# An encoder trunk on one core: the queue that stores kept differences, where down's first inputs are split, and three more seven-product pairs

## The chip, the cores and the metric

The kernel runs on one core of a Trainium2 chip. The metric is the device time of one execution in microseconds (us), less is better. The kernel before takes 2078.95 us, the median of three executions that took 2076.1, 2078.95 and 2083.54 us.

## What is computed

Two encoder layers over 256 tokens of width 2048, with an MLP of width 8192. Both layers have an attention sub-layer (differential attention in the first, windowed grouped attention in the second, each with four heads into a memory of 256 tokens) and a squared-ReLU MLP:

```python
for i in range(2):
    h = rms_norm(x, norm_attn[i])
    ...                                  # projections, attention, memory attention
    x = x + heads @ w_out[i]             # 2048 x 2048
    h = rms_norm(x, norm_mlp[i])
    x = x + jnp.square(jax.nn.relu(h @ w_up[i])) @ w_down[i]     # 2048 x 8192, 8192 x 2048
```

The change touches the MLP alone, which the kernel runs as a stage "up" (`h @ w_up`) and a stage "down".

## The kernel before, in words

**Products.** The matmuls take operands of a reduced type (`F32R`), so each float32 operand is split into a high part (a cast on ScalarE, ACT in the profile, line 442) and a low part (a subtraction on VectorE, DVE, line 443). One product is then three matmuls on TensorE (PE), high by high, high by low and low by high, each 128x128 by 128x512 (`three`, lines 534 to 536). Weights arrive in pieces of 128x1024. Two pieces make a pair, and a pair of plain form is eight products, so 24 matmuls.

**Seven-product pairs.** Some pairs are computed with seven products (`seven`, 21 matmuls) in the manner of Strassen. Such a pair, called fast here, needs sums of weights, which `sum_pair` makes on VectorE (lines 356 and 357, and `first_sum`, line 283) and splits into four parts `ah, al, bh, bl`; and differences of the inputs, which `differences` makes on VectorE (lines 545 to 548) and splits as well. `FAST` and `LATE` list which of the 32 pairs of each half of down are fast: `LATE` holds for the second half of the first layer's down, `FAST` for the three others. `LATE_BLK` lists those of `LATE` whose sums lie in the buffers `blk` and not in `x2`. The first sum of a fast pair in down is made ahead in DRAM by `make_sums`, with a copy (line 291) and an accumulating transfer (line 295) that GpSimd (POOL) issues while earlier stages run.

**Kept differences.** The input differences of a fast pair serve both halves of down. They are made once, while up makes the hidden values: `keep` takes a buffer `h2`, makes the differences, and stores them to DRAM in a transfer that GpSimd issues (line 1013). Down loads them again for each half (`load_kept`, line 1122, GpSimd). Hidden chunks 6 to 14 are also moved to DRAM by GpSimd (line 1037) and loaded by SyncE (SP).

**Order.** The program's text is not the order of the engines alone. Tasks such as `keep` are queued with a wait counted in ticks; the loop over pairs gives two ticks with each pair, at which due tasks are emitted (`Light(f, gap)` runs `f`, and the next step of the task follows `gap` ticks later). Buffers come from pools: `x2` has 8, `h2` 6, `blk` 10. A buffer is handed out again in turn, so an instruction that writes to a handed-out buffer waits until the last reader of it is done, a storing DMA among these. Each engine executes its instructions strictly in its own order, so whatever stands behind a waiting one waits too.

**Start of down.** Up ends with its last pair, the side sums `u`, and `to_hidden`, which transposes them on PE (line 1031) and applies relu and square on ScalarE (lines 1033, 1034). Down then splits its first input in `h2_of(0)` and starts.

Of the kernel before, what the change touches and what calls it, by code (L numbers as in the profile page):

```python
# [15 lines left out]
F32R = mybir.dt.float32r  # L16
# [6 lines left out]
P = 128  # L23
# [24 lines left out]
AHEAD = 2  # L48
WARM = 10
FAST = (2, 4, 6, 7, 9, 11, 12, 14, 16, 17, 19, 21, 22, 24, 26, 27, 29)  # L50
LATE = (2, 4, 6, 9, 11, 12, 14, 16, 19, 21, 24, 26, 29)
AWAY = range(6, 15)
LATE_BLK = (9, 12, 16, 21, 26)
LOOK = 3
KEEP_AFTER = (2, 6, 10, 14)
KEEP_LAST = (10, 18, 26, 34)
SUM_AT = {0: 44, 1: 2}
SUM_GAP = ({"in": 4, "mem": 4, "out": 4, "up": 11}, {"in": 4, "mem": 12, "out": 12, "up": 7})
LAM_INIT = 0.8 - 0.6 * math.exp(-0.3 * 0)
# [11 lines left out]
def trunk(ctx: ExitStack, tc: tile.TileContext, xin, xtok, memin, memtok, posrel, gcol, rows,  # L71
# [12 lines left out]
    def nm(s):  # L84
        uid[0] += 1
        return f"{s}{uid[0]}"
# [4 lines left out]
    def quad(tag, shape=(P, 2, 2, 256), dt=F32R):  # L91
        return xp.tile(list(shape), dt, tag=tag, name=nm(tag), bufs={"x2": 8, "h2": 6, "blk": 10}[tag])
# [904 lines left out]
    def mlp(layer, X2, last):  # L997
# [7 lines left out]
        def hidden(j):  # L1005
            return hT[j // 2].rearrange("p k s -> p (k s)")[:, (j % 2) * 512:(j % 2) * 512 + 512]

        def keep(j):

            t2 = quad("h2", (P, 2, 512))  # L1010
            differences(t2, hidden(j))
            kept[j] = dp.tile([P, 2, 512], F32R, name=nm("kept"))
            nc.gpsimd.dma_start(kept[j], t2)

        name = f"up{layer}"
        diffs = {}
# [6 lines left out]
        def to_hidden(q, n, u, i, tag):  # L1023
            c = 2 * q + n
            if i == 0:
                hT.append(wide[:, 5] if c == 15 else blk([P, 4, S], F32))
            pt = bank(tag)
            for oo in range(2):
                for t in range(2):
                    o = 2 * i + oo  # L1030
                    nc.tensor.transpose(out=pt[:, oo * S + t * P:oo * S + (t + 1) * P], in_=u[n][t][:, o * P:(o + 1) * P], identity=ident)  # L1031
            j = 2 * c + i
            nc.scalar.activation(hidden(j), pt, AF.Relu)
            nc.scalar.activation(hidden(j), hidden(j), AF.Square)
            if c in AWAY:
                hidden_in[j] = dp.tile([P, 512], F32, name=nm("hid"))
                nc.gpsimd.dma_start(hidden_in[j], hidden(j))
            if any(j in fast_pairs(f"down{layer}", h) for h in range(2)):
                Task([Light(lambda: keep(j), 0)], wait=KEEP_AFTER[2 * n + i] if q < 7 else KEEP_LAST[2 * n + i])

        for q in range(8):
            tag, other = ("mm", "aux") if q % 2 == 0 else ("aux", "mm")
            own = [[bank(tag) for _ in range(2)] for _ in range(2)]
            fast = UP_FAST[q]
            for j in range(8):
                if j == fast[0]:
                    side = [bank(other) for _ in range(4)]
                if q == 0 and j in DIFF_UP:
                    i = DIFF_UP[j]
                    diffs[i] = quad("h2" if i == 2 else "blk", (P, 2, 512))  # L1050
                    pair_differences(X2.pairs[i], diffs[i])
                two = [piece(name, q, 2 * j + i) for i in range(2)]
                pair = X2.pairs[j]

                def at(kk, t, part):
                    return pair[:, kk, part, t * P:(t + 1) * P]

                if j in fast:
                    seven(own, side, j == fast[0], j == fast[-1], two, sums.pop((name, q, j)), at, diffs[j])
                elif j < 7:  # L1060
                    for kk in range(2):
                        for t in range(2):
                            for n in range(2):
                                one_of_eight(own, n, t, 2 * j + kk, KT - 1, two, at)
                else:
                    for n in range(2):
                        for t in range(2):
                            for kk in range(2):
                                one_of_eight(own, n, t, 2 * j + kk, KT - 1, two, at)
                if j == fast[-1]:  # L1070
                    u = side_sums(side)
                for _ in range(2):
                    tick(2)
            own_add(own, u)
            if q == 0:
                mlp_stats()
            Task([lambda q=q, u=u, n=n, i=i, tag=tag: to_hidden(q, n, u, i, tag) for n in range(2) for i in range(2)], wait=1, gap=0)
        slots.append(blk([P, 4, S], F32))
        N2 = Halves()
        while making:  # L1080
            making.popleft()[1]()

        def h2_of(j):
            t2 = quad("h2", (P, 2, 512))
            split(t2[:, 0, :], t2[:, 1, :], hids.pop(j) if j in hidden_in else hidden(j))
            return lambda kk, t, part: t2[:, part, kk * S + t * P:kk * S + (t + 1) * P]

        for half_ in range(2):
            tag = "mm" if half_ == 0 else "aux"
# [32 lines left out]
                    nc.gpsimd.dma_start(diff_in[j], kept[j])  # L1122

            load_kept(1)
            ats = deque([h2_of(0)])
            for j in range(32):
                if j == fast[0]:
                    side = [bank("aux" if half_ == 0 else "mm") for _ in range(4)]
                two = [piece(f"down{layer}", half_, 2 * j)]
                if j < 31:  # L1130
                    ats.append(h2_of(j + 1))
                load_kept(j + 2)
                two.append(piece(f"down{layer}", half_, 2 * j + 1))
                at = ats.popleft()
# [184 lines left out]
```

## Time and profile before

| what | value |
|---|---|
| median of three executions | 2078.95 us |
| the profiled execution | 2079.43 us |
| its span in the profile | 2077.6 us, so 1.83 us lie outside it |
| TensorE busy, and its mean granted clock | 2068.8 us, 1.0 |
| VectorE, ScalarE, GpSimd busy | 1790.4, 1280.2, 193.2 us |
| DMA | 572.28 MB, mean 275 GB/s |
| up of the first layer, and of the second | about 404 to 764 us, 1402 to 1748 us |
| down of the first layer, first and second half | about 764 to 938 us, 938 to 1100 us |
| down of the second layer | about 1748 to 2077 us |

A row of a timeline gives the start in us, the duration, the engine, the line, the operation, and output<-inputs by the program's names, with partitions by elements. In brackets stands the engine's idle time just ahead of the row and what released it. A matmul is listed with 0.39 us, but matmuls overlap, so the distance between starts is what each costs. A row of the table by stretch holds the busy time of each engine in that stretch with the count of instructions, then the granted clock, the DMA share and GB/s. Rows of DMA issues give the count, the size and the median us from issue to landing.

### The profile page before, as it was taken

To read this page: it belongs to the slowest core of one execution; us is meant where nothing else is said; L and a number is where in the kernel's file an instruction comes from. 1 tells how busy PE (TensorE), PEld (TensorE's weight loads), DVE (VectorE), ACT (ScalarE), POOL (GpSimd) and SP (SyncE) were. 2 spreads that over 40 slices of the span, in tenths; PEclk is the share of its full clock that TensorE was granted. 3 is DMA by queue.
4 is the path that set the end of the run, shared out by engine and by line. 5 is a ranking of instruction groups with operands and counts; after the bars stand their busy time and mean duration, and the time that the engine had idled before them with its cause. 6 is when DMAs were issued, how large, how long until landed. Compare 5 with 4: busy or idle time off the path is not lost.

```text
span 2077.6 us, 28751 instructions
## 1 busy us (share of the span) xinstructions
PE 2068.8 (100%) x9996; PEld 1718.0 (83%) x9996; DVE 1790.4 (86%) x2583; ACT 1280.2 (62%) x1906; POOL 193.2 (9%) x301
## 2 busy tenths in 40 slices
PE   9999999999999999999999999999999999999999
PEld 7888888888888888888888888888888888888887
DVE  7677778898999999998886678889999889999998
ACT  7466665556655676666655556566556567766764
POOL 1201111100010010000001110000101111000000
PEclk9999999999999999999999999999999999999999
DMA  9678988877887789988978987568889998998994
GB/s 312 244 241 276 272 291 232 269 232 218 272 291 259 237 293 329 357 289 282 326 265 273 267 252 228 187 223 244 262 273 293 303 286 309 328 363 309 306 356 168
DMA packets 170641, 572.28 MB, mean 275 GB/s; under 512 B 19744, under 2 KB 20768, under 8 KB 169248
## 3 DMA queue, kind: packets, MB, share of 16 engines
q1 hardware_dynamic: 132976, 440.41, 59.8%
q0 software_dynamic: 37376, 130.04, 23.4%
q8 instruction: 78, 1.28, 0.2%
q14 instruction: 67, 0.55, 0.1%
q10 hardware_dynamic: 144, 0.01, 0.0%
HBM read 537.74 MB, written 97.65 MB: 306 GB/s over the span
## 4 chain that ended last, share of the span: by engine, by line
PE 92%; DMA 2%; DVE 2%; issue 2%; ACT 1%; SPq 0%; POOL 0%; ACTq 0%; DVEq 0%; POOLq 0%
PE mm L535 11%; PE mm L534 11%; PE mm L536 11%; PE aux L535 11%; PE aux L536 11%; PE aux L534 11%; PE mm L495 7%; PE mm L496 7%; PE mm L497 7%; DMA kept<-h 1%; DVE lo L443 1%; PE aux L638 1%; PE mm L1031 1%; PE aux L615 1%; PE aux L657 1%
## 5 line engine op out<-in xcount | busy, mean ns | idle before, releaser
L443 DVE TENSOR_TENSOR lo<-raw,hi 128x1024 fp32r<-128x1024 f32 (+1 forms) x512 | 607.6, 1207 | 168.3 <-ACT hi L442 166.7
L442 ACT CAST hi<-raw 128x1024 fp32r<-128x1024 f32 (+1 forms) x512 | 515.3, 1036 | 377.7 <-PE mm L497 113.9
L495 PE MATMUL mm<-hi,x 128*128 128x512 f32 x640 | 256.7, 403 | 0.7 <-ACT hi L442 0.7
L496 PE MATMUL mm<-lo,x 128*128 128x512 f32 x640 | 250.8, 392 | 0.0
L497 PE MATMUL mm<-hi,x 128*128 128x512 f32 x640 | 250.3, 391 | 0.0
L442 ACT CAST h<-big 128x1024 fp32r<-128x1024 f32 (+1 forms) x100 | 101.1, 1020 | 145.0 <-DVE big L283 90.2
L535 PE MATMUL aux<-lo,h 128*128 128x512 f32 x440 | 171.5, 390 | 0.2 <-DVE lo L443 0.2
L534 PE MATMUL aux<-hi,h 128*128 128x512 f32 x440 | 171.6, 390 | 0.0
L536 PE MATMUL aux<-hi,h 128*128 128x512 f32 x440 | 171.4, 389 | 0.0
L534 PE MATMUL mm<-hi,h 128*128 128x512 f32 (+1 forms) x438 | 170.1, 389 | 0.9 <-ACT h L442 0.9
L535 PE MATMUL mm<-lo,h 128*128 128x512 f32 (+1 forms) x438 | 169.8, 388 | 0.0
L536 PE MATMUL mm<-hi,h 128*128 128x512 f32 (+1 forms) x438 | 169.5, 388 | 0.0
L534 PE MATMUL mm<-hi,x 128*128 128x512 f32 x414 | 161.9, 391 | 0.0
L535 PE MATMUL mm<-lo,x 128*128 128x512 f32 x414 | 161.5, 390 | 0.2 <-DVE lo L443 0.2
L536 PE MATMUL mm<-hi,x 128*128 128x512 f32 x414 | 161.3, 390 | 0.0
L442 ACT CAST hi<-big 128x1024 fp32r<-128x1024 f32 (+1 forms) x146 | 128.9, 911 | 47.8 <-issue 24.5
L535 PE MATMUL aux<-lo,x 128*128 128x512 f32 x398 | 155.3, 390 | 0.5 <-DVE lo L443 0.5
L534 PE MATMUL aux<-hi,x 128*128 128x512 f32 x398 | 155.7, 391 | 0.0
L536 PE MATMUL aux<-hi,x 128*128 128x512 f32 x398 | 155.1, 390 | 0.0
L443 DVE TENSOR_TENSOR lo<-big,hi 128x1024 fp32r<-128x1024 f32 (+1 forms) x146 | 149.1, 1044 | 4.3 <-ACT hi L442 4.3
L497 PEld LDWEIGHTS mm<-hi,x 128*128 128x128 f32 x640 | 120.2, 188 | 26.0
L495 PEld LDWEIGHTS mm<-hi,x 128*128 128x128 f32 x640 | 120.5, 189 | 24.6 <-ACT hi L442 1.1
(310 smaller groups left out, 4268.6 us busy)
## 6 DMA issues: line engine op xcount, KB each, us to landing
raw<-in_w_up SPq DMA_DIRECT2D x164, 512.0 KB, 5.8
raw<-in_w_down SPq DMA_DIRECT2D x128, 512.0 KB, 5.6
madesum<-in_w_down POOLq DMA_DIRECT2D x124, 512.0 KB, 6.5
big<-in_w_up SPq DMA_DIRECT2D x92, 512.0 KB, 4.6
raw<-in_w_a SPq DMA_DIRECT2D x72, 512.0 KB, 4.7
h<-kept POOLq DMA_DIRECT2D x64, 512.0 KB, 5.9
big<-in_w_down SPq DMA_DIRECT2D x54, 512.0 KB, 5.2
big<-madesum SPq DMA_DIRECT2D x53, 512.0 KB, 5.3
```

The lines of the kernel that those rows point to most:

```text
L442: nc.scalar.copy(hi, src)
L443: return nc.vector.tensor_tensor(lo, src, as32(hi), op=ALU.subtract)
L495: nc.tensor.matmul(ps[t], lhsT=xh, rhs=hi[:, ws], start=(k == 0), stop=False)
L496: nc.tensor.matmul(ps[t], lhsT=xh, rhs=lo[:, ws], start=False, stop=False)
L497: nc.tensor.matmul(ps[t], lhsT=xl, rhs=hi[:, ws], start=False, stop=(k == KT - 1))
L534: nc.tensor.matmul(acc_, lhsT=x(0), rhs=w2[0][:, ws], start=first_, stop=False)
L535: nc.tensor.matmul(acc_, lhsT=x(0), rhs=w2[1][:, ws], start=False, stop=False)
L536: nc.tensor.matmul(acc_, lhsT=x(1), rhs=w2[0][:, ws], start=False, stop=last_)
L615: nc.tensor.transpose(out=pt[:, h * P:(h + 1) * P], in_=qn[t][:, h * P:(h + 1) * P], identity=ident)
L638: nc.tensor.transpose(out=pt[:, kt * S + qt * P:kt * S + (qt + 1) * P], in_=p_of(qt)[:, kt * P:(kt + 1) * P], identity=ident)
L657: nc.tensor.matmul(ps[c][:, qt * S:(qt + 1) * S], lhsT=qT[a][r, hl, qs], rhs=kT[b][r, hl, :], start=(a + b == 0), stop=(a == 1))
L1031: nc.tensor.transpose(out=pt[:, oo * S + t * P:oo * S + (t + 1) * P], in_=u[n][t][:, o * P:(o + 1) * P], identity=ident)
```

## The change

Three edits, all in the MLP.

First, `LATE` goes from 13 to 16 pairs: 17, 22 and 27 are added, so that the second half of the first layer's down has fast pairs next to each other at 16 and 17, 21 and 22, 26 and 27, as the other halves have. All halves together go from 64 to 67 fast pairs. `LATE_BLK` is chosen anew. The built program has 9 matmuls fewer, 6 casts more on ScalarE and 12 operations more on VectorE; six more transfers make the three sums in DRAM, three more load them and three more load kept differences.

Second, `keep` makes the differences as before, but the store is a step of its own, two ticks (one pair) later, and ScalarE issues it (`nc.scalar.dma_start`, line 1017 of the changed kernel) instead of GpSimd. There are 34 such stores.

Third, the first input of each half of down is split sooner. That of the first half, `h2_of(0)`, is emitted at the last pair of up (q = 7, j = 7), before its pieces; that of the second half at the last pair of the first half.

```diff
-LATE = (2, 4, 6, 9, 11, 12, 14, 16, 19, 21, 24, 26, 29)
+LATE = (2, 4, 6, 9, 11, 12, 14, 16, 17, 19, 21, 22, 24, 26, 27, 29)
-LATE_BLK = (9, 12, 16, 21, 26)
+LATE_BLK = (9, 12, 16, 19, 22, 26, 29)
+KEEP_GAP = 2
...
-        def keep(j):
-
-            t2 = quad("h2", (P, 2, 512))
-            differences(t2, hidden(j))
-            kept[j] = dp.tile([P, 2, 512], F32R, name=nm("kept"))
-            nc.gpsimd.dma_start(kept[j], t2)
+        def keep(j, wait):
+
+            def make():
+                box.append(quad("h2", (P, 2, 512)))
+                differences(box[0], hidden(j))
+
+            def store():
+                kept[j] = dp.tile([P, 2, 512], F32R, name=nm("kept"))
+                nc.scalar.dma_start(as32(kept[j]), as32(box.pop()))
+
+            box = []
+            Task([Light(make, KEEP_GAP), Light(store, 0)], wait=wait)
...
-                Task([Light(lambda: keep(j), 0)], wait=KEEP_AFTER[2 * n + i] if q < 7 else KEEP_LAST[2 * n + i])
+                keep(j, KEEP_AFTER[2 * n + i] if q < 7 else KEEP_LAST[2 * n + i])
...
+                if q == j == 7:
+                    ats = deque([h2_of(0)])
                 two = [piece(name, q, 2 * j + i) for i in range(2)]
...
-            ats = deque([h2_of(0)])
             for j in range(32):
...
-                if j < 31:
-                    ats.append(h2_of(j + 1))
+                if j < 31 or half_ == 0:
+                    ats.append(h2_of((j + 1) % 32))
```

What moves on the engines is seen at three places. In the names, `hi` and `lo` are the parts of a weight piece, `h2` and `x2` the buffers of those pools, `mm` and `aux` the accumulators, `big`, `t2k` and `raw` float32 buffers that hold sources, `kept` the stored differences in DRAM.

TensorE at the start of the first layer's down, before: the transposes of up's last hidden chunks (of 16, the last four), then the first plain pair.

```order
L1031 MATMUL aux1666_7865<-ident_76,t2k1633_7729 128x128
L1031 MATMUL aux1666_7865<-ident_76,t2k1635_7731 128x128
L1031 MATMUL aux1666_7865<-ident_76,t2k1633_7729 128x128
L1031 MATMUL aux1666_7865<-ident_76,t2k1635_7731 128x128
L534 MATMUL mm1646_7787<-hi1637_7738,h21650_7791 128x512
L535 MATMUL mm1646_7787<-lo1638_7739,h21650_7791 128x512
L534 MATMUL mm1648_7789<-hi1640_7744,h21650_7791 128x512
```

The same place after: up's last matmuls into `aux`, and the first pair of down behind them.

```order
L535 MATMUL aux1565_7404<-hi1628_7700,x2997_4764 128x512
L536 MATMUL aux1565_7404<-lo1629_7701,x2997_4764 128x512
L537 MATMUL aux1565_7404<-hi1628_7700,x2997_4764 128x512
L535 MATMUL mm1649_7797<-hi1641_7750,h21639_7746 128x512
L536 MATMUL mm1649_7797<-lo1642_7751,h21639_7746 128x512
L537 MATMUL mm1649_7797<-hi1641_7750,h21639_7746 128x512
```

The 16 transposes now stand behind these 24 matmuls. The second layer has the same order.

ScalarE in the first half of the first layer's down, about 50 us in, before: casts of weights (`hi`), of sums (`x2`) and of inputs (`h2`).

```order
L442 CAST hi1757_8282<-big979_4686 128x1024
L442 CAST hi1766_8303<-t2k1730_8150 128x512
L442 CAST h21776_8351<-t2k1759_8284 128x512
L442 CAST h21784_8391<-t2k1771_8337 128x512
L442 CAST x21762_8290<-big979_4686 128x1024
L442 CAST x21772_8341<-big979_4686 128x1024
L442 CAST hi1768_8331<-big979_4686 128x1024
```

The same place after, with the store of the last kept differences (`h21757`).

```order
L443 CAST hi1759_8289<-big979_4686 128x1024
L443 CAST hi1768_8310<-t2k1733_8159 128x512
L1017 DMA kept1770_8338<-h21757_8282 128x1024
L443 CAST h21779_8360<-t2k1761_8291 128x512
L443 CAST x21764_8297<-big979_4686 128x1024
L443 CAST h21787_8400<-t2k1774_8346 128x512
L443 CAST x21775_8350<-big979_4686 128x1024
```

`h21787` is handed the buffer that `h21757` leaves, so its cast waits until the store has landed, with two casts between. In the kernel before, it is a load on GpSimd that takes over the stored buffer. The second layer has such a place as well.

GpSimd in up of the second layer, before: stores of kept differences stand between the copy and the accumulation of the sums that are made ahead.

```order
L295 DMA madesum3230_14947<-in_w_down 256x1x512
L1013 DMA kept3211_14864<-h23209_14857 128x1024
L291 DMA madesum3264_15092<-in_w_down 16x8192
L295 DMA madesum3264_15092<-in_w_down 256x1x512
L1013 DMA kept3257_15077<-h23255_15070 128x1024
```

ScalarE at the last of these stores, after (the same chunk of differences is `h23270` here).

```order
L443 CAST h23270_15106<-t2k3271_15107 128x512
L443 CAST hi3273_15114<-raw3272_15113 128x1024
L443 CAST hi3276_15120<-raw3275_15119 128x1024
L1017 DMA kept3279_15149<-h23270_15106 128x1024
L443 CAST hi3280_15151<-big2978_13737 128x1024
L443 CAST hi3282_15155<-big2978_13737 128x512
L443 CAST h23284_15162<-big2978_13737 128x1024
L443 CAST h23286_15164<-big2978_13737 128x1024
```

The store stands behind no accumulation any more, but behind two casts. The buffer it leaves is written again by the subtraction of a low part `bl` on VectorE; before, it was written by the cast of `bh` on ScalarE, which stands one step earlier.

More of the change, by code (lines that the diff above doesn't have):

```diff
@@ L1006, in hidden, with h2_of @@
             return hT[j // 2].rearrange("p k s -> p (k s)")[:, (j % 2) * 512:(j % 2) * 512 + 512]
-        def keep(j):
+        def keep(j, wait):
[7 more added lines that the diff above has]
+            Task([Light(make, KEEP_GAP), Light(store, 0)], wait=wait)
+        def h2_of(j):
             t2 = quad("h2", (P, 2, 512))
-            differences(t2, hidden(j))
-            kept[j] = dp.tile([P, 2, 512], F32R, name=nm("kept"))
-            nc.gpsimd.dma_start(kept[j], t2)
+            split(t2[:, 0, :], t2[:, 1, :], hids.pop(j) if j in hidden_in else hidden(j))
+            return lambda kk, t, part: t2[:, part, kk * S + t * P:kk * S + (t + 1) * P]
         name = f"up{layer}"
@@ L1081, in mlp @@
             making.popleft()[1]()
-        def h2_of(j):
-            t2 = quad("h2", (P, 2, 512))
-            split(t2[:, 0, :], t2[:, 1, :], hids.pop(j) if j in hidden_in else hidden(j))
-            return lambda kk, t, part: t2[:, part, kk * S + t * P:kk * S + (t + 1) * P]
         for half_ in range(2):
```

## The prediction

> **What bounds the kernel now.** I read the totals of the page, its chain of waits, the table by stretch for the stage that is given more work, and then timelines at the places where TensorE waits. The totals and the engines' shares of the chain:
>
> ```profile
> PE 2068.8 (100%) x9996; PEld 1718.0 (83%) x9996; DVE 1790.4 (86%) x2583; ACT 1280.2 (62%) x1906; POOL 193.2 (9%) x301
> PE 92%; DMA 2%; DVE 2%; issue 2%; ACT 1%; SPq 0%; POOL 0%; ACTq 0%; DVEq 0%; POOLq 0%
> ```
>
> TensorE is the bound, and 8% of the chain lies elsewhere. So two things shorten the time: fewer matmuls, and fewer waits of TensorE. The two halves of the first layer's down, in the table by stretch (stretch, its us, then busy us and count of PE, PEld, DVE, ACT, POOL, granted clock, DMA share, GB/s):
>
> ```profile
> 764.00:938.00 174.00, 173.33 (x774) 143.75 (x773) 163.15 (x199) 122.21 (x165) 11.69 (x22) 1.00 0.93 326
> 938.00:1100.00 162.00, 161.82 (x718) 133.62 (x717) 137.10 (x158) 99.62 (x128) 11.43 (x15) 1.00 0.83 286
> ```
>
> The first half has 17 fast pairs and VectorE at 163.15 of 174 us, and TensorE is short of full by 0.67 us only; the second half has 13, and VectorE at 137.10 of 162 us. There is room where the pairs are added.
>
> TensorE's timeline in up of the second layer, at the costliest wait; a steady stretch stands ahead of it:
>
> ```profile
> 1559.70 0.39 PE L535 MATMUL aux<-lo,blk 128*128 128x512 f32 x1
> ...
> 1560.83 0.39 PE L534 MATMUL mm<-h,blk 128*128 128x512 f32 x1
> 1561.06 0.39 PE L535 MATMUL mm<-h,blk 128*128 128x512 f32 x1
> 1561.28 0.39 PE L536 MATMUL mm<-h,blk 128*128 128x512 f32 x1
> 1561.95 0.50 PE L534 MATMUL mm<-h,blk 128*128 128x512 f32 x1 [0.28 <-ACT h L442]
> 1563.21 0.50 PE L535 MATMUL mm<-h,blk 128*128 128x512 f32 x1 [0.76 <-DVE h L443]
> 1563.54 0.39 PE L536 MATMUL mm<-h,blk 128*128 128x512 f32 x1
> 1563.77 0.39 PE L534 MATMUL aux<-h,x 128*128 128x512 f32 x1
> ```
>
> From 1559.70 to 1561.28 there are seven distances, 0.226 us each: that is a matmul's price, not the 0.39 us of its row, which overlaps the next. From 1560.83 to 1563.77 six distances take 2.94 us in place of 1.36, so this wait costs 1.58 us, more than its brackets say.
>
> **Fewer matmuls.** Three more fast pairs take away 9 matmuls, 9 x 0.226 = 2.03 us, all on the path. What they add lies on other engines:
>
> ```profile
> L443 DVE TENSOR_TENSOR x<-big,x 128x1024 fp32r<-128x1024 f32 x100 | 121.8, 1218 | 1.1 <-ACT x L442 1.0
> L443 DVE TENSOR_TENSOR lo<-raw,hi 128x1024 fp32r<-128x1024 f32 x496 | 597.1, 1223 | 166.7 <-ACT hi L442 165.1
> L443 DVE TENSOR_TENSOR h<-t2k,h 128x512 fp32r<-128x512 f32 x108 | 72.9, 685 | 1.5 <-ACT h L442 1.3
> L356 DVE TENSOR_TENSOR big<-big 128x512 f32<-128x512 f32 x78 | 53.7, 689 | 1.5
> ```
>
> A plain pair takes VectorE two weight splits and one input split, 2 x 1.22 + 0.69 = 3.13 us. A fast pair needs two sum splits (2 x 1.22), two additions (2 x 0.69), and of its second piece only half is split, which makes 1.22 + 0.69 + 2.44 + 1.38 + 0.69 = 6.42 us. That is 3.3 us more per pair, 9.9 us for three: VectorE goes to 147 of some 160 us, 92%, where the first half ran at 94% with the same adjacent couples 16 and 17, 21 and 22, 26 and 27. Its cover is the plain pairs around the couples; if that is gone, it costs what the third rival says. ScalarE's six casts and the transfers (DMA share 0.83, against 0.93 in the first half) get no price for the same reason.
>
> **Start of down.** Up's end in both layers, rows of TensorE's timeline:
>
> ```profile
> 764.83 0.50 PE L534 MATMUL mm<-hi,h 128*128 128x512 f32 x1 [0.67 <-ACT h L442]
> ...
> 1747.79 0.98 PE L1031 MATMUL aux<-ident,t2k 128*128 128x128 f32 x7 [0.29 <-DVE t2k L1021]
> 1748.95 0.50 PE L534 MATMUL mm<-hi,h 128*128 128x512 f32 x1 [0.19 <-ACT h L442]
> ```
>
> TensorE waits for the last side sums (`t2k`), then for the first input split. Afterwards 24 matmuls that need neither stand ahead of the transposes: 24 x 0.226 = 5.4 us, in which VectorE makes the sums. So 0.67 + 0.29 + 0.19 = 1.15 us go; if restarts are shortened too, up to 1.6. What is late next is nothing that the rows show. The sooner split for the second half removes no wait of the table, and counts nothing.
>
> **Stores out of GpSimd's queue.** Two more places of up in the second layer, TensorE's timeline:
>
> ```profile
> 1642.04 0.39 PE L534 MATMUL aux<-hi,x 128*128 128x512 f32 x1
> 1642.96 0.50 PE L535 MATMUL aux<-lo,x 128*128 128x512 f32 x1 [0.53 <-DVE lo L443]
> ...
> 1643.53 0.40 PE L534 MATMUL aux<-hi,x 128*128 128x512 f32 x1
> ...
> 1694.30 0.40 PE L534 MATMUL aux<-h,blk 128*128 128x512 f32 x1
> 1695.41 0.50 PE L535 MATMUL aux<-h,blk 128*128 128x512 f32 x1 [0.71 <-DVE h L443]
> ...
> 1698.85 0.39 PE L534 MATMUL mm<-hi,x 128*128 128x512 f32 x1
> ```
>
> Three distances take 1.49 us in place of 0.68 (0.81 lost), and twelve, from 1694.30 to 1698.85, take 4.55 in place of 2.71 (1.84 lost). Together with the first place, 4.23 us. At all three, ScalarE stands still shortly before, in its timeline:
>
> ```profile
> 1560.85 1.05 ACT L442 CAST h<-big 128x1024 fp32r<-128x1024 f32 x1 [5.92 <-DMA kept<-h]
> ...
> 1640.07 0.62 ACT L442 CAST h<-t2k 128x512 fp32r<-128x512 f32 x1 [2.07 <-DMA kept<-h]
> ...
> 1693.04 1.05 ACT L442 CAST h<-big 128x1024 fp32r<-128x1024 f32 x1 [5.32 <-DMA kept<-h]
> ```
>
> Its cast writes to a buffer that a store still reads. Why the store is late, by GpSimd's timeline, the chain, and the DMA issues of two windows, that of this store and one with a store behind no accumulation:
>
> ```profile
> 1547.01 1.08 POOL L295 DMA_DIRECT2D madesum<-in_w_down  x1 [6.08 <-DMA madesum<-in_w_down]
> 1548.91 0.56 POOL L1013 DMA_DIRECT2D kept<-h  x1 [0.82 <-DVE h L443]
> 1548.91 11.84 DMA kept<-h
> kept<-h POOLq DMA_DIRECT2D x1, 512.0 KB, 6.2
> ```
>
> The store comes right behind an accumulating transfer and lands after 11.84 us; another, with none ahead, after 6.2. The change takes the store to another queue, about one pair later, which gives away some of that; but the buffer's next writer also stands one step later (by the order, 35 matmuls or 7.9 us behind the store at the nearest in up), and a store of 6.2 us is inside. I take the whole 4.23 us; the other end is nothing (first rival).
>
> The Trainium skill (DMA: Bandwidth & Descriptors, "Issuing engines are not separate DMA queues") says that transfers from any engine run on the same 16 DMA engines and interleave, so that another issuer saves only its issuing time. By that rule the 4.23 us would stay; the same page's "Queues, rings and completion order" lets each DMA engine take turns between queue rows, which would let the store pass the accumulation. The 6.2 and 11.84 us do not decide between these two.
>
> The added store waits on ScalarE for VectorE's subtraction. Behind it stand the casts of weights. On GpSimd that wait was 0.82 us with no gap; the gap of one pair (21 x 0.226 = 4.7 us) covers it. Issuing cost GpSimd 0.56 us a store; 34 of them are 19 us, in some 800 us that ScalarE is idle: nothing.
>
> **A new wait in down.** The last store of each layer has its buffer written again two casts later, by ScalarE itself. ScalarE's timeline at this place before, and the DMA issues of the first half:
>
> ```profile
> 814.15 0.62 ACT L442 CAST hi<-t2k 128x512 fp32r<-128x512 f32 x1
> 815.49 1.30 ACT L442 CAST h<-t2k 128x512 fp32r<-128x512 f32 x2 [0.72 <-PE aux L536]
> 816.70 2.00 ACT L442 CAST x<-big 128x1024 fp32r<-128x1024 f32 x2
> 820.97 1.06 ACT L442 CAST hi<-big 128x1024 fp32r<-128x1024 f32 x1 [2.27 <-issue]
> raw<-in_w_down SPq DMA_DIRECT2D x32, 512.0 KB, 5.9
> kept<-h POOLq DMA_DIRECT2D x2, 512.0 KB, 7.7
> ```
>
> The store is issued at about 814.8 and lands 5.9 us later by SyncE's row, at 820.7. ScalarE is through with the casts between at about 817.7 and waits 3.0 us; 2.27 us of idle follow there that can take it up, so 0.7 remain. The nearest row for such a remainder is the wait of 2.07 us, which cost 0.81. I take 0.5 us a layer, 1.0 in all; the ends are 0 and 1.84 (the wait of 5.32 us) a layer.
>
> **The sum.** 2079.43 - 2.03 - 1.15 - 4.23 + 1.00 = 2073.02 us for the profiled execution. That one lay 0.48 us above the median of the runs shown, so against the median I forecast 2072.5 us. Its own range: both new waits free and 1.6 us at the starts give 2071.1; both at 1.84 give 2075.2.
>
> **Rivals.**
>
> First, *the stores gain nothing*: a store lands late wherever it is issued, because the accumulation and the loads fill the DMA engines. For it speaks, from the DMA issues while that store is under way, that SyncE's loads are as slow:
>
> ```profile
> raw<-in_w_up SPq DMA_DIRECT2D x2, 512.0 KB, 9.7
> ```
>
> Against it, the next writer stands later in any case. The 4.23 us come back: 2076.8 us.
>
> Second, *ScalarE is held by its own stores*: they land after 7.7 us and more, and casts wait behind. Both places in down cost 1.84 (2.68 more than taken), and at three in up a short wait of the 0.81 kind stays (2.43): 2077.7 us. Against it, 35 matmuls in up.
>
> Third, *VectorE becomes the bound in the second half of the first layer's down*, and the kernel ends slower. A fast pair takes VectorE 6.42 us and TensorE 4.75, so 1.67 are missing per pair; in three adjacent couples, six pairs, 10 us, if VectorE has no lead at their starts: 2082.5 us. It decides from a lead below 2 x 1.67 = 3.3 us a couple. Against it, the first half ran such couples at 173.33 of 174 us; for it, the new `LATE_BLK` hands out `blk` and `x2` in another turn, which no row of before shows.
>
> **How the numbers follow.** Chances: the forecast 0.68, the first rival 0.17, the second 0.09, the third 0.06. A measurement of this kernel can tell about 0.3% from no change, 6.2 us, so faster means below 2072.7. The forecast lies right there: of its 0.68 I put 0.43 below and 0.25 above, since several waits of ScalarE on these stores were not priced and the new wait was. Both first rivals count as the same; of the third I put half beyond 0.3%, for further waits in its train. Faster 0.43, same 0.25 + 0.17 + 0.09 + 0.03 = 0.54, slower 0.03. The range goes from the forecast's low end, less half of the 2.85 us by which the lowest run lies below the median (2069.7), to just above the second rival (2078.0); outside it are the third rival and about 0.1 more.
>
> **What would show it.** Right, if in the profile after TensorE has 9 matmuls fewer, no bracket at the start of down, and at none of up's three places ScalarE's wait for `kept`; if the stores from ScalarE's queue land in about 6 us; and if at the last store ScalarE's cast waits some 3 us and TensorE below 1. Wrong, if the stores land in 10 us or more (first rival), if ScalarE's rows wait for `kept` in up (second), or if TensorE waits for VectorE's `x` or `lo` between 938 and 1100 us (third).

## The result and the profile after

The changed kernel takes 2071.61 us, the median of six executions (2070.87 to 2072.4); the kernel before took 2079.91 us beside it, the median of six (2076.1 to 2083.54). The ratio is 0.9962, with a 95% interval of 0.9951 to 0.9973: the interval lies clear of 1, so the kernel is faster, and the median is 0.9 us below the forecast. The profiled execution took 2070.87 us, its span is 2069.1 us.

The page of the changed kernel, totals and the engines' shares of the chain:

```profile
PE 2063.2 (100%) x9987; PEld 1715.1 (83%) x9987; DVE 1792.3 (87%) x2595; ACT 1283.8 (62%) x1912; POOL 179.9 (9%) x276
PE 97%; DVE 2%; DMA 1%; issue 0%; ACT 0%; SPq 0%; ACTq 0%; DVEq 0%
```

TensorE ran 9 instructions fewer, and its share of the chain went from 92 to 97%: most of what was gained is waiting. To see where, I cut both spans at the same points of TensorE's program (first matmul of a stage, first transpose of a group) and compared the pieces:

| piece | before, us | after, us | difference |
|---|---|---|---|
| start to the first transposes of the first layer's up | 464.94 | 464.37 | -0.57 |
| from there to the transposes of its seventh column block | 259.48 | 259.48 | 0 |
| end of up and first half of down | 210.18 | 209.20 | -0.98 |
| second half of down | 160.52 | 159.64 | -0.88 |
| second layer, to its up's first transposes | 348.88 | 348.69 | -0.19 |
| from there to its up's seventh transposes | 264.39 | 259.48 | -4.91 |
| end of up and all of down | 366.09 | 364.92 | -1.17 |
| behind the last matmul | 3.11 | 3.33 | +0.22 |

That is -8.5 us, all of the difference between the spans. The piece with the largest gain, in the table by stretch, before:

```profile
1444.02:1708.41 264.39, 261.87 (x1196) 215.84 (x1195) 237.06 (x287) 156.44 (x199) 35.52 (x52) 1.00 0.88 281
```

and after:

```profile
1441.37:1700.85 259.48, 259.48 (x1195) 216.32 (x1194) 236.10 (x288) 156.59 (x200) 28.03 (x39) 1.00 0.89 288
```

TensorE is now busy for all of the 259.48 us, as long as the same piece of the first layer took in both kernels. The start of down, in TensorE's timeline after:

```profile
766.86 0.39 PE L537 MATMUL mm<-hi,h 128*128 128x512 f32 x1
767.09 1.91 PE L1043 MATMUL aux<-ident,t2k 128*128 128x128 f32 x16
768.75 0.48 PE L535 MATMUL mm<-hi,h 128*128 128x512 f32 x1
```

Nothing waits there any more, and the 16 transposes take 1.66 us from the first start to the next matmul. Before, they took 2.60 (762.23 to 764.83 us).

The new waits that came are in the second half of the first layer's down. The costlier one, in TensorE's timeline:

```profile
1041.53 0.39 PE L535 MATMUL aux<-hi,h 128*128 128x512 f32 x1
1042.45 0.50 PE L536 MATMUL aux<-lo,h 128*128 128x512 f32 x1 [0.53 <-DVE lo L444]
1042.79 0.39 PE L537 MATMUL aux<-hi,h 128*128 128x512 f32 x1
1043.02 0.39 PE L535 MATMUL aux<-hi,h 128*128 128x512 f32 x1
```

Three distances take 1.49 us in place of 0.68: 0.8 us lost 108 us into the half, because VectorE splits this piece late. Another such wait, 98 us in, loses 0.3. Both follow a place where VectorE itself had nothing to do, by the timelines of ScalarE and VectorE:

```profile
1026.98 1.05 ACT L443 CAST blk<-big 128x1024 fp32r<-128x1024 f32 x1 [5.07 <-DMA big<-madesum]
...
1029.01 2.36 DVE L444 TENSOR_TENSOR lo<-raw,hi 128x1024 fp32r<-128x1024 f32 x2 [4.60 <-ACT hi L443]
```

ScalarE stood 5.07 us for the load of a sum made ahead. SyncE issued that load only at 1020.82 us, when VectorE had just finished with the buffer that it fills. The casts of the next weights stand behind that cast on ScalarE, so VectorE stood idle for 4.60 us; from 1029.01 us on it works without a pause and is late at both waits.

### The profile page after: what moved, and what is told of

Its sections match the earlier page's. It is cut to its first block, busy times and chain, and to the rows that moved or that the text cites. A ratio compares the mean times of both kernels' runs of the same rounds, so it can differ in the third digit from the quotient of the medians.

```text
span 2069.1 us, 28771 instructions
## 1 busy us (share of the span) xinstructions
PE 2063.2 (100%) x9987; PEld 1715.1 (83%) x9987; DVE 1792.3 (87%) x2595; ACT 1283.8 (62%) x1912; POOL 179.9 (9%) x276
## 4 chain that ended last, share of the span: by engine, by line
PE 97%; DVE 2%; DMA 1%; issue 0%; ACT 0%; SPq 0%; ACTq 0%; DVEq 0%
PE mm L536 12%; PE mm L537 12%; PE mm L535 12%; PE aux L536 11%; PE aux L537 11%; PE aux L535 11%; PE mm L496 7%; PE mm L497 7%; PE mm L498 7%; DVE lo L444 1%; PE aux L639 1%; PE mm L1043 1%; PE aux L1043 1%; PE aux L616 1%; PE aux L658 1%; PE aux L696 1%
## 5 line engine op out<-in xcount | busy, mean ns | idle before, releaser
L443 ACT CAST hi<-raw 128x1024 fp32r<-128x1024 f32 (+1 forms) x506 | 509.6, 1036 | 355.4 <-PE mm L498 109.4
L444 DVE TENSOR_TENSOR lo<-raw,hi 128x1024 fp32r<-128x1024 f32 (+1 forms) x506 | 600.5, 1203 | 148.8 <-ACT hi L443 147.4
L536 PE MATMUL aux<-lo,h 128*128 128x512 f32 x422 | 164.6, 390 | 0.7 <-DVE lo L444 0.7
L535 PE MATMUL aux<-hi,h 128*128 128x512 f32 x422 | 164.4, 390 | 0.0
L537 PE MATMUL aux<-hi,h 128*128 128x512 f32 x422 | 164.2, 389 | 0.0
L498 PEld LDWEIGHTS mm<-hi,x 128*128 128x128 f32 x640 | 120.2, 188 | 26.0
L444 DVE TENSOR_TENSOR h<-big,h 128x1024 fp32r<-128x1024 f32 (+1 forms) x100 | 116.4, 1179 | 28.7 <-ACT h L443 26.4
```

Of the source, the lines that this page charges most:

```text
L443: nc.scalar.copy(hi, src)
L444: return nc.vector.tensor_tensor(lo, src, as32(hi), op=ALU.subtract)
L498: nc.tensor.matmul(ps[t], lhsT=xl, rhs=hi[:, ws], start=False, stop=(k == KT - 1))
L535: nc.tensor.matmul(acc_, lhsT=x(0), rhs=w2[0][:, ws], start=first_, stop=False)
L536: nc.tensor.matmul(acc_, lhsT=x(0), rhs=w2[1][:, ws], start=False, stop=False)
L537: nc.tensor.matmul(acc_, lhsT=x(1), rhs=w2[0][:, ws], start=False, stop=last_)
```

## The experiments

Most of these kernels differ from execution to execution more than the changed one (the kernel before: 2074.6 to 2082.7 us in 33). So beside the medians I read the pieces of the table above, which in stages without waits repeat to 0.1 us. A piece comes from the one profiled execution. Where stages wait it varies too: with the stores on GpSimd, the piece of the second layer's up takes 264.39 us in the kernel before, 263.57 in `e1_pairs`, 263.31 in `e2_sooner` and 262.24 in `e4_no_stores`.

**One edit at a time.** `e1_pairs` is the kernel before with the new `LATE` and `LATE_BLK`:

```diff
-LATE = (2, 4, 6, 9, 11, 12, 14, 16, 19, 21, 24, 26, 29)
+LATE = (2, 4, 6, 9, 11, 12, 14, 16, 17, 19, 21, 22, 24, 26, 27, 29)
-LATE_BLK = (9, 12, 16, 21, 26)
+LATE_BLK = (9, 12, 16, 19, 22, 26, 29)
```

> The three pairs alone (LATE and LATE_BLK as in the changed kernel, everything else as before). My theory: 9 matmuls go (2.0 us), and VectorE is late at two places of the first layer's second half of down, which takes back 1.1 us, whatever queue stores the differences: about 0.9 us below the kernel before, so 2079.0 us beside 2079.9, with TensorE waits of 0.3 and 0.8 us in that half and up's three waits of 4.2 us untouched. Rival: those two waits come from what stores on ScalarE's queue or the sooner split moved; then the half shows none and the kernel comes 2.0 us down, 2077.9.

Measured: 2078.84 us beside 2078.76, ratio 1.0 (0.9991 to 1.0009). The time tells nothing; the trace does: the half takes 159.97 us (160.52 before), with waits of 0.36 us at 98 and 0.82 us at 108 us into it. They belong to the pairs, not to the stores or the splits.

`e2_sooner` is the kernel before with `h2_of` as in the changed kernel (the two places of `ats` in the diff above).

> The sooner first splits alone. My theory: the waits at the start of both layers' down go, 1.0 us in the first layer and 1.2 in the second by the spans of these stages in the two traces: 2.2 us, so 2077.7 us beside 2079.9, and up's three waits stay. Rival: part of what the stages gained there comes from the stores that left GpSimd (the last one lies at the start of down); then the gain is 1.15 us or less, 2078.8.

Measured: 2077.44 us beside 2078.76 (ratio 0.9999, 0.999 to 1.0008): no difference that the times can tell. By pieces: the end of up and the first half of down 209.20 us (-0.98), the second layer's 365.06 (-1.03). So the sooner split alone brings 2.0 us in these traces, where the brackets that I had added up came to 1.15.

`e3_stores` is the kernel before with `keep` as in the changed kernel.

> The stores alone: a step later and from ScalarE's queue; pairs and first splits as before. My theory: up of the second layer loses its three waits and the small ones in their train, 4.9 us by the spans of the stage in the two traces: 2075.0 us beside 2079.9, with no wait of ScalarE for a kept store in up. Rival: the waits went with the other edits' shift of the order, and come back here: 2077 us or more.

Measured: 2076.43 us beside 2078.76 (ratio 0.9993, 0.9984 to 1.0002), between the times of the theory and of the rival, and only 1.5 us from the fastest to the slowest of 11 executions. The piece of up takes 259.48 us, -4.91, as expected. But the ends of up became longer, 210.86 us (+0.68) and 366.57 (+0.48). TensorE's timeline at the start of down in this kernel:

```profile
763.04 1.13 PE L1043 MATMUL aux<-ident,t2k 128*128 128x128 f32 x8 [0.42 <-DVE t2k L1033]
764.44 0.33 PE L1043 MATMUL aux<-ident,t2k 128*128 128x128 f32 x1 [0.27 <-DVE t2k L1033]
764.96 0.50 PE L535 MATMUL mm<-hi,h 128*128 128x512 f32 x1 [0.19 <-ACT h L443]
```

Here VectorE's side sums are later than before. With 24 matmuls ahead of the transposes, as in the changed kernel, that lateness costs nothing: the edits help each other, and their single gains in time don't add up to the whole.

`e4_no_stores` is the changed kernel with `keep` as before, so the second edit undone:

```diff
-        def keep(j, wait):
...
+        def keep(j):
+
+            t2 = quad("h2", (P, 2, 512))
+            differences(t2, hidden(j))
+            kept[j] = dp.tile([P, 2, 512], F32R, name=nm("kept"))
+            nc.gpsimd.dma_start(kept[j], t2)
```

> The changed kernel with the stores as before (GpSimd, no step between); pairs and sooner splits stay. If the edits add up, 4.9 us come back: 2076.5 us beside 2071.6, with the three waits in up of the second layer as in the kernel before, at ScalarE's cast behind a kept store. If the waits were a matter of the general order, they are gone here too: 2071.6.

Measured: 2074.82 us beside 2078.76 (ratio 0.9983, 0.9974 to 0.9992), 2072.25 to 2077.98. The piece of up takes 262.24 us, and ScalarE waits again, by the table of waits from 1440 to 1705 us:

```profile
ACT h L442 <- DMA kept<-h: 9.7, 3, 5.4
```

Neither expectation came out: TensorE lost 1.9 us at the third of the three places, next to nothing at the other two, and 0.8 at a place that the kernel before doesn't have, 51 us into the piece. The stores are worth 3.2 us by the medians (2074.82 to 2071.61), 2.8 by this trace's piece, though its execution was one of the slower (2076.87 us).

**Queue, gap, kind of transfer, buffer.** In `e5_syncE` SyncE issues the stores, in `e6_no_gap` ScalarE does without the two ticks:

```diff
-                nc.scalar.dma_start(as32(kept[j]), as32(box.pop()))
+                nc.sync.dma_start(as32(kept[j]), as32(box.pop()))
```

```diff
-KEEP_GAP = 2
+KEEP_GAP = 0
```

> The changed kernel with the 34 stores issued by SyncE instead of ScalarE. SyncE's queue has no accumulating transfers either, but all weight loads. The buffer's next writer stands 88, 26 and 29 matmuls behind the store at the three places of up (19.9, 5.9 and 6.6 us). My theory, that a store is slow because it stands behind an accumulation: it lands in 6 to 8 us, ScalarE waits at most 2 us at the second and third place, up of the second layer loses less than 1 us, 2071.6 to 2073. Rival, that the time until the buffer is written decides: the second and third place lose what they lost in the kernel before, about 2.6 us: 2074. Second rival, that a store that waits for VectorE holds up the weight loads behind it on SyncE: casts wait for raw, slower than 2075.

Measured: 2072.13 us beside 2078.05 (ratio 0.9976, 0.9967 to 0.9986), with single executions up to 2075.97. The piece of up takes 260.41 us; none of the three old places waits, though the next writer stands only 26 and 29 matmuls behind at two of them. ScalarE's longest wait for a kept store is 2.4 us. The 0.9 us are lost 51 us into the piece, the place that `e4_no_stores` has as well.

> The changed kernel with the gap of two ticks taken away (KEEP_GAP = 0): ScalarE stores right behind the differences. The next writer is 36, 35 and 36 matmuls behind. My theory: the queue does it, not the gap: up of the second layer takes the same 259.5 us from its second chunk's first transposes to its last, and the kernel 2071.6 us. Rival: without the gap ScalarE waits for VectorE's subtraction, the casts of weights behind it come late, and each of the 34 stores costs a little: above 2073 us.

Measured: 2071.63 us (ratio to before 0.9968, 0.9957 to 0.998), the piece of up 259.48 us. The gap does nothing; the queue does, or the later turn of the buffer that comes with it (36, 35 and 36 matmuls against 31, 23 and 31 in `e4_no_stores`).

`e7_plain` is `e4_no_stores` with a plain transfer in place of each accumulating one, which leaves out the second summand of the sums that are made ahead:

```diff
-            nc.gpsimd.dma_start(made_in[name, h, j], upper.unsqueeze(1).broadcast_to([P, 2, 512]), accum_op=ALU.add)
+            nc.gpsimd.dma_start(made_in[name, h, j], upper.unsqueeze(1).broadcast_to([P, 2, 512]))
```

> The stores on GpSimd as before, pairs and first splits as in the changed kernel, and in place of each accumulating transfer a plain one of the same size on the same queue. The sums that are made ahead are not sums then, which leaves out that part of the computation. Theory: accumulating is what holds up the store behind it; with plain transfers a store lands in 6 to 7 us, ScalarE's waits for kept stores shrink below 2 us and up of the second layer takes 259.5 us. Rival: any large transfer ahead on that queue holds the store up; stores keep landing after 10 us and more, and the stage takes 262 to 264 us as with accumulations.

Measured: 2070.54 us (ratio to before 0.9967, 0.9956 to 0.9979), the piece of up 259.48 us, with the stores on GpSimd and the buffers in the old turn. DMA issues from 1400 to 1760 us (count, KB, median us to landing), of the kernel before:

```profile
madesum<-in_w_down POOLq DMA_DIRECT2D x32, 512.0 KB, 6.9
kept<-h POOLq DMA_DIRECT2D x16, 512.0 KB, 8.6
```

of `e7_plain`:

```profile
madesum<-in_w_down POOLq DMA_DIRECT2D x32, 512.0 KB, 5.9
kept<-h POOLq DMA_DIRECT2D x16, 512.0 KB, 7.1
```

and of the changed kernel:

```profile
madesum<-in_w_down POOLq DMA_DIRECT2D x32, 512.0 KB, 7.0
kept<-h ACTq DMA_DIRECT2D x16, 512.0 KB, 7.7
```

ScalarE still waits for a kept store in `e7_plain`, longer than the 2 us of my theory, but never long enough for TensorE to notice:

```profile
ACT h L442 <- DMA kept<-h: 6.7, 3, 3.4
```

So it is not GpSimd's queue as such that costs, but the accumulating transfers. Without them the DMA engines also have less to do (the transfers for the sums land after 5.9 us, not 6.9), so this run does not tell a store that stands behind an accumulation from one that runs beside it. The landings of the 34 stores tell more:

| kernel | stores issued by | went out while an accumulation was under way: median, longest us | with no transfer for sums under way: median us |
|---|---|---|---|
| before | GpSimd | 9.3, 11.8 | 6.0 |
| `e4_no_stores` | GpSimd | 8.9, 11.2 | 5.7 |
| changed | ScalarE | 8.2, 8.9 | 5.3 |
| `e6_no_gap` | ScalarE | 8.3, 10.8 | 5.3 |
| `e5_syncE` | SyncE | 7.6, 10.1 | 5.0 |
| `e7_plain` | GpSimd, plain transfer under way instead | 7.3, 9.5 | 5.6 |

Under way means issued and not yet landed when the store went out. Beside an accumulation a store is some 3 us late on any queue. On GpSimd's queue, behind the accumulation, it lands about 1 us later than on ScalarE's, and half of that shows in the last column too.

`e8_later_turn` is `e4_no_stores` with seven buffers `h2` in place of six and, since the memory holds no more, nine `blk` in place of ten:

```diff
-        return xp.tile(list(shape), dt, tag=tag, name=nm(tag), bufs={"x2": 8, "h2": 6, "blk": 10}[tag])
+        return xp.tile(list(shape), dt, tag=tag, name=nm(tag), bufs={"x2": 8, "h2": 7, "blk": 9}[tag])
```

> The stores on GpSimd as before, accumulations as before, pairs and first splits as in the changed kernel, but seven buffers h2 (and nine blk): the next writer of a stored buffer comes 36, 66 and 33 matmuls behind the store (8.2, 15, 7.5 us) where it came 31, 23 and 31 behind, much as in the changed kernel (35 each). Theory, the queue: stores still land after 10 us and more, so waits of 1 to 3 us for them stay at the first and third place and up of the second layer takes 260.5 to 262 us. Rival, the buffer's turn alone: the waits are gone, and the stage takes 259.5 us.

Measured: 2110.06 us (ratio to before 1.0158, 1.0141 to 1.0175). The missing `blk` makes TensorE wait for hidden values in every up, up to 6.6 us at a time, and this covers what the run was meant to show; it decides nothing on the stores.

`e12_own_buffer` asks the same without that cost: `e4_no_stores`, with the differences of three pairs in a part of `big` that lies idle during up.

```diff
-            t2 = quad("h2", (P, 2, 512))
+            if j in (9, 17, 21):
+                t2 = wide[:, 5].rearrange("p a s -> p (a s)").rearrange("p (a n) -> p a n", a=2).bitcast(F32R)
+            else:
+                t2 = quad("h2", (P, 2, 512))
```

> The stores on GpSimd as before, accumulations as before, pairs and first splits as in the changed kernel; but the differences of pairs 9, 17 and 21 are made in a part of the buffer big that up leaves unused until its end, so that the next writer of every stored buffer in up comes 42 matmuls (9.5 us) or more behind the store, at most places 47 (10.6 us) or more. Theory, that a late store costs time only through the writer of its buffer: stores behind an accumulation still land after 10 us and more, but up of the second layer takes 259.5 us as with ScalarE's queue, and the kernel 2071.6 us, 3 us below the same with the buffers in the old turn (2074.8). Rival, that accumulation and store together also slow what else is on the DMA engines: the stage stays at 261 us and more.

Measured: 2073.25 us beside 2078.91 (ratio 0.997, 0.9961 to 0.9979), 1.6 us below `e4_no_stores`. At the three old places TensorE waits no more, with store and accumulation on the same queue. But the piece takes 261.43 us, because of a fourth place, in TensorE's timeline:

```profile
1492.94 0.39 PE L536 MATMUL aux<-hi,x 128*128 128x512 f32 x1
1493.91 0.50 PE L534 MATMUL mm<-hi,x 128*128 128x512 f32 x1 [0.58 <-ACT hi L442]
1494.64 0.50 PE L535 MATMUL mm<-lo,x 128*128 128x512 f32 x1 [0.22 <-DVE lo L443]
```

Some 20 us earlier, by the DMA issues from 1466 to 1476 us, two transfers for the sums, a store and six loads go out close together:

```profile
raw<-in_w_up SPq DMA_DIRECT2D x4, 512.0 KB, 11.1
big<-in_w_up SPq DMA_DIRECT2D x2, 512.0 KB, 5.8
madesum<-in_w_down POOLq DMA_DIRECT2D x2, 512.0 KB, 9.6
kept<-h POOLq DMA_DIRECT2D x1, 512.0 KB, 11.1
```

SyncE's loads into `raw` land as late as the store. ScalarE stood 6.2 us and then 3.0 us for two of them, and its casts and VectorE's splits stayed behind until 1494 us. So both theories have a share: at the three places the cost comes through the buffer's writer, and the crowd on the DMA engines can also cost where no buffer is shared. The fourth place is not peculiar to this run. By distances between starts it costs 1.4 us in `e1_pairs`, 0.6 in `e2_sooner`, 0.8 in `e4_no_stores` and the 0.9 of `e5_syncE`, and nothing in the kernel before, in `e7_plain` and where ScalarE issues the stores. Whether the accumulation or the store brings it is not shown.

**The pairs.** Three variants of the second half of the first layer's down, all with the rest as in the changed kernel: a 17th pair (`LATE = FAST`, so 7 is added); 7 in the place of 22; and other pairs in `blk`.

```diff
-LATE = (2, 4, 6, 9, 11, 12, 14, 16, 17, 19, 21, 22, 24, 26, 27, 29)
+LATE = FAST
```

```diff
-LATE = (2, 4, 6, 9, 11, 12, 14, 16, 17, 19, 21, 22, 24, 26, 27, 29)
+LATE = (2, 4, 6, 7, 9, 11, 12, 14, 16, 17, 19, 21, 24, 26, 27, 29)
-LATE_BLK = (9, 12, 16, 19, 22, 26, 29)
+LATE_BLK = (9, 12, 16, 19, 26, 29)
```

```diff
-LATE_BLK = (9, 12, 16, 19, 22, 26, 29)
+LATE_BLK = (9, 12, 16, 17, 21, 24, 27)
```

> The changed kernel with a 17th fast pair, 7, in the second half of the first layer's down. Theory, that the new waits there belong to the couples at 19 to 22, where VectorE makes the sums of the next pair before it splits the piece that TensorE wants: pair 7 stands elsewhere, its 3 matmuls (0.7 us) come off, the waits 98 and 108 us into the half stay, the half takes 159.0 us beside 159.64, the kernel 2070.9. Rival, that VectorE's work in all is at its limit there: another 3.3 us of it bring new waits near pairs 6 and 7 that cost 0.7 us and more: 2071.6 or slower.

> The changed kernel with still 16 fast pairs in that half, but 7 in the place of 22 (and 22 out of LATE_BLK). Theory, the couples: with pair 22 plain VectorE has no sums to make ahead of the piece of pair 21, the wait of 0.7 to 0.8 us at 108 us into the half goes, the half takes 158.8 us beside 159.64, the kernel 2070.8. Rival, VectorE's work in all: the same wait shows at this place or another, 159.6 us, 2071.6.

> The changed kernel with another choice of the pairs whose sums lie in blk: 17, 21, 24 and 27 in place of 19, 22, 26 and 29. Theory, VectorE's work near the couples: the waits at 98 and 108 us into the half stay, 159.6 us, 2071.6 for the kernel. Rival, the turn of the buffers: ScalarE and SyncE wait for buffers in use at 19 and 22 and the sums come late for this alone; with the other choice the waits go and the half takes 158.5 us, 2070.5.

Measured: `e9_seventeen` 2072.28 us (ratio to before 0.9972, 0.9962 to 0.9981), up to 2076.88; `e10_swap` 2071.58 us (0.9967, 0.9955 to 0.998); `e11_other_blk` 2073.21 us (0.9976, 0.9967 to 0.9986). The half in the table by stretch, in the kernel before, which has 13 pairs:

```profile
934.61:1095.13 160.52, 160.34 (x708) 132.32 (x707) 136.22 (x159) 98.14 (x125) 10.35 (x14) 1.00 0.84 288
```

in the changed kernel, with 16:

```profile
933.05:1092.68 159.63, 158.90 (x699) 130.41 (x698) 141.97 (x169) 102.51 (x130) 11.33 (x17) 1.00 0.85 300
```

in `e10_swap`, with another 16:

```profile
934.72:1093.14 158.42, 158.17 (x699) 130.64 (x698) 143.65 (x169) 103.10 (x131) 12.01 (x17) 1.00 0.87 302
```

and in `e9_seventeen`:

```profile
933.91:1095.92 162.01, 159.14 (x696) 129.60 (x695) 147.33 (x173) 104.72 (x133) 12.07 (x18) 1.00 0.86 300
```

Without 22, the waits at 98 and 108 us are gone and the half is 2.1 us shorter than with 13 pairs, the whole worth of 9 matmuls. One wait of 0.5 us, 56 us in, is new there, and one of nearly 0.6, 21 us in, that the kernel before and the changed one both have, is not. `e11_other_blk` keeps the couple at 21 and 22 and changes only the buffers (`e10_swap` changes pairs and buffers): its waits at 98 and 108 us are gone as well, and one of 0.76 us comes at 133 us, near pair 26. My theory for that run, that they stay, fell. So the couple alone is not the cause; it costs with this choice of buffers.

What the waits have in common is the place that the section on the profile after shows. In all seven traces with the changed kernel's pairs and buffers ScalarE stands 4.75 to 5.65 us for a sum's load 94 us into the half, and VectorE stands idle 4.15 to 4.75 us with it. In `e10_swap` and `e11_other_blk` neither happens there. Where they have such a stand of over 4 us instead, their new wait of TensorE follows: the stand ends at 976.4 us and the wait at 991.9 in `e10_swap`, at 1051.7 and 1067.2 in `e11_other_blk`, where the changed kernel has 1027.0 and 1042.5. It is 15.5 us each time. Why the sum's load comes late there I did not trace further back than to the buffer that it fills.

`e9_seventeen` decides less. Its profiled execution has waits at six places, and its half is longer than with 13 pairs; but it took 2076.88 us, the longest of twelve, and six of the twelve took 2070.66 to 2071.76, as short as the changed kernel's. What the half takes in those is not on record. None of the variants beats the changed kernel by its median. `e10_swap` comes out at the time of its rival though its half goes as the theory had it: of what it gains there, the profiled execution lost 0.66 us to a wait in the first half (209.88 us in place of 209.20). Whether the edit brings that wait, through the sums that are made ahead, is not shown.

## Why the prediction was right, step by step

**Stores, -4.23 us: right in kind; -4.91 between the two traces, 3.2 by the medians.** The three waits are gone; 0.68 more were small waits in their train, which the sum left out. That the size came so close is partly luck. The prediction read it from one execution, and of the four traces with stores on GpSimd this one loses most in the piece (4.91 us against 2.8 to 4.1 in the others), not always at the same places.

The reason held in part. The prediction counted on a store that lands in 6.2 us, inside the 7.9 us until the next writer of its buffer, and named "about 6 us" as a sign. At the three places the stores land after 8.6, 8.2 and 8.9 us (11.8, 8.1 and 11.2 before), so at the second the queue changed nothing. The delay got smaller, the writer comes later, and what is left falls on VectorE, in the changed kernel's table of waits from 1440 to 1705 us:

```profile
DVE h L444 <- DMA kept<-h: 1.5, 1, 1.5
```

TensorE does not wait for it. Either part was nearly enough by itself: `e5_syncE` removes the three waits by the queue, with the writer hardly later at two places, and `e12_own_buffer` removes them by the buffer, with the queue as before. Of the rule from the Trainium skill (DMA: Bandwidth & Descriptors, "Issuing engines are not separate DMA queues"), that another issuer saves only its issuing time: the times speak against it for a store behind an accumulation (2074.82 us on GpSimd, 2071.61 on ScalarE, 2072.13 on SyncE). The landings agree with it for the larger part, since stores beside accumulations stay late on another queue (8.2 us against 5.3). With plain transfers ahead (2070.54 us) the rule's answer would have been the right one. So the first rival is out as to the time. The second is out as well: with no gap at all ScalarE's queue costs TensorE nothing.

**Start of down, -1.15 us: right in kind, too small.** Measured -2.0 alone (`e2_sooner`), and -2.15 beside the stores, above my bound of 1.6. I added brackets, where I had shown earlier in the same text that brackets say less than the distances between starts. By starts the transposes took 2.60 us in both layers where 1.66 are enough.

**Nine matmuls, -2.03 us with all extra work hidden: the step that failed.** The half gained 0.88 us. VectorE's load was as estimated or below (141.97 of 159.63 us, 89%, against 147 and 92%), and yet 1.1 us were lost. The prediction asked how much VectorE has to do and not when its inputs come: VectorE stood idle for 4.60 us behind ScalarE's wait of 5.07 us for a sum's load, and then had the sums of the couple ahead of the split that pair 21 wants. Other buffers with the same pairs (`e11_other_blk`) and other pairs (`e10_swap`) have neither the stand nor these two waits. That the first half runs the same couples was no proof; its buffers come in another turn. The sign that the prediction named for its third rival, TensorE waiting for VectorE's `lo` between 938 and 1100 us, is there. It is that rival by its sign and at 1.1 us, not 10, and by another way than VectorE's load, since VectorE had time left.

**The new wait in down, +1.00 us: not there.** ScalarE's timeline at the second layer's place:

```profile
1788.65 1.04 ACT L443 CAST hi<-big 128x1024 fp32r<-128x1024 f32 x1
1788.96 0.33 ACTq L1017 DMA_DIRECT2D kept<-h  x1
1789.60 0.61 ACT L443 CAST hi<-t2k 128x512 fp32r<-128x512 f32 x1
1791.62 0.62 ACT L443 CAST h<-t2k 128x512 fp32r<-128x512 f32 x1 [1.41 <-PE mm L537]
1792.14 1.05 ACT L443 CAST x<-big 128x1024 fp32r<-128x1024 f32 x1
1794.29 0.62 ACT L443 CAST h<-t2k 128x512 fp32r<-128x512 f32 x1 [1.09 <-DMA kept<-h]
```

The store went out at 1788.96 us, 0.64 before the cast behind which it stands in the order had even begun, where I had let it wait for that cast's end: 1.3 us sooner. It landed at 1794.29 us, after 5.3. ScalarE waited 1.09 us, not 3, and TensorE not at all. The first layer has the same cast:

```profile
818.20 0.62 ACT L443 CAST h<-t2k 128x512 fp32r<-128x512 f32 x1 [2.01 <-DMA raw<-in_w_down]
```

The bracket names a load, but the store landed at 818.12 us, 6.2 after it went out, and it is the store that this cast waits for. TensorE did not wait here either, after 2.01 us of ScalarE's idle; the row of 2.07 us that the prediction priced at 0.81 was no measure for this place.

**The sum.** Against the forecast for the profiled execution (2073.02 us) the measured 2070.87 is 2.15 us lower: 1.15 too much for the matmuls, and 0.68, 1.0, and 1.0 too little for the stores, the starts and the wait, and some 0.6 in pieces that the change doesn't touch. The errors of the terms, 1.15 one way and 2.68 the other, cancelled in part, and that is luck. By the medians, each beside its own measurement of the kernel before, 6.45 us were forecast and 8.3 came.

## What to carry to other kernels

A store that goes out beside an accumulating transfer lands some 3 us late here on any queue, and later still when it stands behind it in the same queue. It costs only where a buffer that it still reads is handed out within that time. So look at what is under way when it goes out and at the buffer's next writer; a later writer and a queue without accumulations each helped.

Price a wait of TensorE by the distances between starts, not by the idle in the brackets, and read more than one execution before taking its waits as the size of a gain.

Cover by total load is no cover. What counts is what stands ahead of the wanted piece in the feeding engine's order and whether that engine had its inputs in time: in these traces the same number of cheaper pairs was worth all of its matmuls or less than half.

## What was not expected of the hardware

A DMA that ScalarE issues does not wait for a cast ahead of it in ScalarE's order, which it doesn't need, to begin: the store went out 0.64 us before that cast in both layers. So the strict order that the description of the kernel gives each engine holds for the casts among themselves, not for such a DMA.

The spread of the times went with the waits, not with the queue alone: 8.2 us over 33 executions of the kernel before, 1.5 us over 11 with the stores moved (`e3_stores`), and 6.2 us over 12 in `e9_seventeen`, which has the stores moved as well and waits in down.

In `e8_later_turn` long waits of TensorE cost more than their length. Its timeline:

```profile
1596.72 0.39 PE L536 MATMUL aux<-h,h 128*128 128x512 f32 x1
...
1602.83 0.80 PE L534 MATMUL aux<-h,h 128*128 128x512 f32 x1 [5.73 <-ACT blk L1038]
1603.43 0.63 PE L535 MATMUL aux<-h,h 128*128 128x512 f32 x1
1603.86 0.63 PE L536 MATMUL aux<-h,h 128*128 128x512 f32 x1
```

and the table by stretch:

```profile
1602.80:1607.20 4.40, 4.37 (x10) 3.48 (x11) 2.94 (x5) 4.40 (x7) 1.07 (x2) 0.50 0.32 120
```

After an idle of 5.7 us the granted clock is 0.50 for 4.4 us, and matmuls start 0.43 us apart in place of 0.226.
